# An output projection whose first four operand rows go through Strassen's seven products, added up in the output's PSUM banks

## The chip, the cores and the metric

One core of one Trainium2 chip runs the whole kernel. The metric is the device time in microseconds (us) from start to end of one execution; the median of three runs is compared. PE is TensorE (matmul), PEld its weight load, DVE is VectorE, ACT is ScalarE, POOL is GpSimd, SP is SyncE, which issues most transfers.

## What is computed

The reference is a trunk of two layers on 512 tokens of width 1024, all in float32. Each layer has a token mixer and a SwiGLU FFN, with normalisation, shift, scale and gate around them. The change is in the second layer's mixer, a Mamba-2 state-space mixer, and there in its last line:

```python
def ssd_mixer(h, w_in, conv_w, conv_b, dt_bias, a_log, d_skip, norm_g, w_out):
    z, xbc, dt_raw = jnp.split(h @ w_in, [M_D_INNER, M_D_INNER + M_CONV_DIM], axis=-1)
...
    y = ssd_chunked(xs, dt, a, bm, cm) + d_skip.reshape(g, r)[:, :, None] * xs
    y = y.reshape(bsz, s, M_D_INNER) * jax.nn.silu(z)
    y = rms_normalize(y.reshape(bsz, s, g, M_D_INNER // g)).reshape(bsz, s, M_D_INNER) * norm_g
    return y @ w_out
```

The mixer works on eight groups of heads; group g gives the columns 256 g to 256 g + 255 of y, so two of the sixteen rows of 128 that the last product sums over.

## The kernel before

**The product.** `y @ w_out` sums over K = 16 rows (blocks of 128). A row k has an operand y_k of 128 x 512 tokens (`ygs[k]`) and a weight row of 128 x 1024. The output is 512 tokens by 1024 columns: two halves of columns (hf 0 and 1) by four token tiles of 128, eight tiles of 128 x 512, and each fills one PSUM bank, of which there are eight: four with the tag mm, four with the tag aux. Half 0 lies in the mm banks, half 1 in the aux banks. Float32 accuracy comes from splitting each operand into a high part, rounded by ACT, and a low part, the rest, by DVE (`split_w` L212 for weights, `y_act` L1959 for y), and three matmuls: high by high, high by low, low by high. So one row costs 8 tiles x 3 matmuls of 128x512 (`mm_tiles`, L381; its matmul is L388).

**Staging.** `out_begin` (L375) makes two generators, one for each half. Each step loads up to four weight rows (`load_wo`, L237) into one of two 8 KB tiles wst, hands out the list of split operations, and on the next step issues the matmuls. The split weights lie in four tiles whl. Half 0 takes rows 0 to 13, half 1 rows 0 to 11; the rest (14, 15 and 12 to 15) are the tail, which the class `Boundary` (L409) issues tile by tile, so that the normalisation and the transposes for the FFN (L509) run between them, in the order written out in `BOUNDARY` (L362). The split y of rows below 12 is made twice, once for each half; those from 12 on are kept.

**The order around it.** The state-space groups run in a software pipeline: the loop over g = 1 to 6 projects group g + 1, finishes group g and normalises group g - 1 (`root`, two ACT functions, and `norm` on DVE). A group's sums of squares come from PE (`sums`, tile ssg in an aux bank) and `root` reads them. `step_a` (L1765) transposes into four aux banks (xtok twice, btokp, cb); `states` takes two, `step_cc` four (yo, yd). After the loop, group 7 is finished among the rows of half 0: rows 0 to 3, `step_a`, rows 4 to 7, `states`, rows 8 to 11, `step_cc`, rows 12 and 13, `sums`; then half 1 and the boundary. In this stretch the text of the kernel gives the order of PE, ACT and DVE up to the last `norm`, and then of PE alone up to the boundary, which again gives all three; otherwise a planner orders the instructions. A tile or bank that is used again waits for the last reader of what was in it.

**Where the memory comes from.** The pool sp holds the group's tiles. When it is closed, a pool bp of 13 tiles of 4 KB takes its place, for the gate, the FFN's first split weights (`load_lead`, L259) and the like. x, which the boundary needs, is loaded again from a copy in HBM into the tiles x0 to x3 behind the loop (L2124).

Of the kernel before, what the change touches and what calls it, by code (L numbers as in the profile page):

```python
# [8 lines left out]
F32 = mybir.dt.float32  # L9
F32R = mybir.dt.float32r  # L10
# [6 lines left out]
P = 128  # L17
T = 512
# [20 lines left out]
def trunk_kernel(  # L39
# [197 lines left out]
    def load_wo(m, hf, k0, nk, later=None, stage=None):  # L237


        src = m[k0 * P:(k0 + nk) * P, hf * T:(hf + 1) * T].rearrange("(k p) f -> p k f", p=P)  # L240
        if stage is None:
            st = wst_p.tile([P, 4, T], F32, tag="wst", name="wsto")
            dma(st[:, :nk, :], src)
        res = []
        for k in range(0, nk, 2):
            w = whl_p.tile([P, 2, 2, T], F32R, tag="whl", name="whlo")
            if stage is None:
                sk = st[:, k:k + 2, :]
# [8 lines left out]
        return res  # L257

    def load_lead(srcs, tile4, later=None):  # L259
# [112 lines left out]
""".split()  # L372
    LATE = 3

    def out_begin(s, w, get_act, K, gg, xn_tile, first, lead, after, stage=None, ys=None, held=None, values=()):  # L375

        ys = [None, None] if ys is None else ys
        held = {} if held is None else held
# [2 lines left out]
        def mm_tiles(hf, ks, tiles, get=get_act):  # L381
            for k, wt, kk in ks:
                a = get(k)
                for t in tiles:
                    tk = slice(t * P, (t + 1) * P)
                    pst = ys[hf][t]
                    for i, (al, wl) in enumerate(((0, 0), (0, 1), (1, 0))):
                        pe.matmul(pst, a[:, al, tk], wt[:, wl, kk, :], start=k == 0 and i == 0,  # L388
                                  stop=k == K - 1 and i == 2, skip_group_check=bool(held))

        def pieces(hf):
            kl = K - (2, 4)[hf]
            k = 0
            while k < kl:
                n = min(4, kl - k)
                ops, acts = [], {}
                ks = load_wo(w, hf, k, n, ops, stage if hf else None)
# [5 lines left out]
                if k == 0:  # L403
# [1221 lines left out]
    with ExitStack() as ph:  # L1625
# [96 lines left out]
        class Group:  # L1722
# [167 lines left out]
            def sums(self):  # L1890
# [4 lines left out]
                else:  # L1895
                    for i in range(2):
                        pe.matmul(self.ssg, ones_r, self.sqs[:, i, :], start=i == 0, stop=i == 1)

            def root(self):
                self.rg = t2("rg")  # L1900
                act.activation(self.rg, self.ssg, AF.Ln, bias=eps_t, scale=1.0 / 256)
                act.activation(self.rg, self.rg, AF.Exp, scale=-0.5)

# [55 lines left out]
        def y_act(k):  # L1959

            if k in split:
                return split[k]
            a = ysp.tile([P, 2, T], F32R, tag="ys", name="ys")
            act.copy(a[:, 0, :], ygs[k])
            dve.tensor_tensor(a[:, 1, :], ygs[k], a[:, 0, :].bitcast(F32), SUB)  # L1965
            if k >= 12:
                split[k] = a
            return a

        gg2, bp = [], []  # L1970
# [4 lines left out]
        def xn_half():  # L1975
            return yp.tile([P, T], F32, tag="y", name="xn")

        parts = out_begin(2, wm_out, y_act, 16, gg2, lambda: (xn_half(), xn_half()), "mm",
                          all_of(ffn_lead(1, tile4b)), ffn_after(1))

        with tc.manual_schedule(engines={PE_ENGINE, mybir.EngineType.Activation, mybir.EngineType.DVE}):
            cur, nxt, nn = Group(0), Group(1), Group(2)
# [81 lines left out]
            for g in range(1, NG - 1):  # L2064
# [34 lines left out]
                if nn:  # L2099
                    nn.weights(0)  # L2100
                    nn.later[0][0]()
                late_fin()
                cur.step_cc()
                nxt.later[5][1]()
# [16 lines left out]
            assert next(steps_late, 0) == 0  # L2121
            for t in range(4):
                xt[t] = hp.tile([P, D], F32, tag=f"x{t}", name=f"x{t}")
                dma(xt[t], x_d[t])  # L2124
# [9 lines left out]
            for op in ops[3:]:  # L2134
                op()
            next(parts[0])
            cur.e_sub(0)
            for op in next(parts[0]):
# [8 lines left out]
            for op in ops[:3]:  # L2147
                op()
            for q in range(2):
                cur.e_mul(q)  # L2150
            for op in ops[3:]:
                op()
            late_fin()
            assert not fins_late or next(fins_late[0], 0) == 0
            ops = next(parts[1])
            for op in ops[:5]:
                op()
# [6 lines left out]
        for op in ops[5:]:  # L2164
            op()
        with tc.manual_schedule(engines={PE_ENGINE}):
            next(parts[1])
            core.close()
            bp.append(ph.enter_context(tc.tile_pool(name="bp", bufs=13, reuse_waits="tile")))
            gg2.append(make_gg(2, lambda: tile4b([P, D], F32, "gg")))  # L2170
            begun = out_finish(parts)

# [434 lines left out]
```

## Time and profile before

| | us |
|---|---|
| median of three runs | 1317.64 |
| lowest, highest | 1317.07, 1319.29 |
| the profiled execution | 1317.96 |
| its span in the profile | 1316.1 |
| PE busy in the span | 1301.8 |
| out-projection's matmuls on PE, first to last start | 874.5 to 972.1 |

The span begins with the first and ends with the last instruction of the profile. A line of a timeline reads: start, duration, engine, line of the kernel, operation, output <- inputs, shape, count; in brackets the idle time before it and what ended it. Neighbouring matmuls overlap, so the time of one is the distance from start to start.

### The profile page before, as it was taken

Reading aid. Unit: us, or ns where it says so; the run is one execution under the profiler, and the core shown is the slowest. Engines: PE = TensorE matmul, PEld = TensorE weight load, DVE = VectorE, ACT = ScalarE, POOL = GpSimd, SP = SyncE. Lnnn points to the kernel's source line nnn. Section 1 sums busy time; section 2 is a strip of 40 time slices with the busy share of each in tenths; the row PEclk is TensorE's granted clock in tenths of the full one; section 3 lists DMA queues with packets and bytes.
Section 4 is the critical chain, followed back from the end, with each engine's and each line's share of the span. In section 5 each row is a group of like instructions: output and inputs, shape, how many; then the busy total and the mean of one; then the engine's idle time right before and its main releaser. Section 6 shows DMA issues by size and latency. Waiting matters only on the chain.

```text
span 1316.1 us, 20444 instructions
## 1 busy us (share of the span) xinstructions
PE 1301.8 (99%) x7865; PEld 1142.9 (87%) x7865; DVE 1020.2 (78%) x1531; ACT 723.4 (55%) x1257; POOL 113.2 (9%) x139
## 2 busy tenths in 40 slices
PE   8999999999999999999999999999999999999998
PEld 6787889999988888898888888888889999998886
DVE  5577857977866986768998998977577777766888
ACT  5332247455532565656775567746574555544665
POOL 0000000111100230000000000000000111101330
PEclk9999999999999999999999999999999999999999
DMA  9767661799868984437664456523342788878871
GB/s 310 229 216 227 218 214 52 196 226 241 202 191 271 257 159 122 139 126 223 216 223 158 145 169 203 176 81 113 111 130 57 195 212 214 198 194 284 178 129 65
DMA packets 225301, 239.06 MB, mean 182 GB/s; under 512 B 10276, under 2 KB 177076, under 8 KB 224180
## 3 DMA queue, kind: packets, MB, share of 16 engines
q1 hardware_dynamic: 204720, 195.10, 47.8%
q0 software_dynamic: 16480, 31.20, 13.4%
q10 hardware_dynamic: 4004, 11.46, 2.6%
q8 instruction: 62, 1.02, 0.3%
q14 instruction: 35, 0.29, 0.1%
HBM read 203.76 MB, written 4.34 MB: 158 GB/s over the span
## 4 chain that ended last, share of the span: by engine, by line
PE 83%; DVE 7%; DMA 4%; ACT 3%; SPq 2%; issue 1%; ACTq 0%; DVEq 0%; POOLq 0%
PE sA L669 12%; PE y L388 8%; PE ip L286 8%; PE ip L288 8%; PE ip L287 8%; PE sC L669 6%; PE cA L2316 4%; PE cA L1327 3%; PE sB L669 3%; PE li L286 2%; PE li L288 2%; PE li L287 2%; DMA ada_st<-in_ada_w_dram 2%; PE li L951 1%; DVE ada_acc L128 1%
## 5 line engine op out<-in xcount | busy, mean ns | idle before, releaser
L286 PE MATMUL ip<-h,whl 128*128 128x512 f32 x640 | 252.6, 395 | 0.2 <-DVE cv L1051 0.2
L288 PE MATMUL ip<-h,whl 128*128 128x512 f32 x640 | 249.3, 390 | 0.0
L287 PE MATMUL ip<-h,whl 128*128 128x512 f32 x640 | 249.2, 389 | 0.0
L286 PEld LDWEIGHTS ip<-h,whl 128*128 128x128 f32 x640 | 120.2, 188 | 25.8 <-issue 1.8
L288 PEld LDWEIGHTS ip<-h,whl 128*128 128x128 f32 x640 | 120.1, 188 | 25.5
L287 PEld LDWEIGHTS ip<-h,whl 128*128 128x128 f32 x640 | 120.2, 188 | 24.0
L669 PE MATMUL sA<-tq,whl 128*128 128x256 f32 x1008 | 130.7, 283 | 0.1
L669 PEld LDWEIGHTS sA<-tq,whl 128*128 128x128 f32 x1008 | 125.4, 192 | 0.6 <-ACT g L679 0.3
L232 DVE TENSOR_TENSOR whl<-wst,whl 128x1024 fp32r<-128x1024 f32 x70 | 85.2, 1220 | 22.9 <-ACT whl L231 22.9
L128 DVE SCALAR_TENSOR_TENSOR ada_acc<-ada_st,csil,ada_acc 128x1024 f32<-128x1024 f32 x70 | 89.8, 1282 | 7.0 <-DMA ada_st<-in_ada_w_dram 5.7
L388 PE MATMUL y<-whlo,ys 128*128 128x512 f32 x384 | 89.6, 392 | 0.2 <-DVE ys L1965 0.2
L388 PEld LDWEIGHTS y<-whlo,ys 128*128 128x128 f32 x384 | 71.7, 188 | 16.4 <-issue 0.6
L286 PE MATMUL li<-h,whl 128*128 128x256 f32 x288 | 83.5, 290 | 0.0
L288 PE MATMUL li<-h,whl 128*128 128x256 f32 x288 | 81.5, 283 | 0.0
L287 PE MATMUL li<-h,whl 128*128 128x256 f32 x288 | 81.4, 283 | 0.0
L231 ACT CAST whl<-wst 128x1024 fp32r<-128x1024 f32 x70 | 72.7, 1040 | 1.8 <-DMA wst<-in_m_w_in_dram 1.8
L1714 DVE SCALAR_TENSOR_TENSOR cu<-ip,cols,cu 128x511 f32<-128x511 f32 (+2 forms) x84 | 62.7, 747 | 3.4 <-ACT cu L1711 1.4
L2316 PE MATMUL cA<-whlo,ao 128*128 128x512 f32 x264 | 61.0, 390 | 0.4 <-DVE w2h L2524 0.2
L2316 PEld LDWEIGHTS cA<-whlo,ao 128*128 128x128 f32 x264 | 49.3, 188 | 11.5 <-ACT whlo L2281 1.2
L286 PEld LDWEIGHTS li<-h,whl 128*128 128x128 f32 x288 | 55.2, 192 | 0.8 <-issue 0.8
L287 PEld LDWEIGHTS li<-h,whl 128*128 128x128 f32 x288 | 55.2, 192 | 0.0
L288 PEld LDWEIGHTS li<-h,whl 128*128 128x128 f32 x288 | 55.1, 191 | 0.0
(397 smaller groups left out, 2649.1 us busy)
## 6 DMA issues: line engine op xcount, KB each, us to landing
ada_st<-in_ada_w_dram SPq DMA_DIRECT2D x96, 512.0 KB, 5.9
wsu<-in_f_w_in_dram SPq DMA_DIRECT2D x30, 512.0 KB, 5.8
sg<-in_f_w_in_dram SPq DMA_DIRECT2D x56, 256.0 KB, 3.6
wsu<-in_f_w_in_dram SPq DMA_DIRECT2D x56, 256.0 KB, 4.8
wst<-in_m_w_in_dram SPq DMA_DIRECT2D x14, 1024.0 KB, 6.3
wst<-in_f_w_in_dram SPq DMA_DIRECT2D x10, 1024.0 KB, 6.3
wst<-in_m_w_in_dram SPq DMA_DIRECT2D x20, 512.0 KB, 4.8
wst<-in_a_w_in_dram SPq DMA_DIRECT2D x9, 1024.0 KB, 7.0
```

The source lines that it names most:

```text
L128: dve.scalar_tensor_tensor(acc, w, csil[:, k:k + 1], acc, MUL, ADD)
L231: later.append((lambda sw=sw, w=w: act.copy(w[:, 0, :nk, :], sw), lambda sw=sw, w=w: dve.tensor_tensor(w[:, 1, :nk, :], sw, w[:, 0, :nk, : ...
L232: lambda sw=sw, w=w: dve.tensor_tensor(w[:, 1, :nk, :], sw, w[:, 0, :nk, :].bitcast(F32), SUB)))
L286: pe.matmul(dst, w_at(w, 0, kk), a[:, 0, sl], start=start, stop=False)
L287: pe.matmul(dst, w_at(w, 0, kk), a[:, 1, sl], start=False, stop=False)
L288: pe.matmul(dst, w_at(w, 1, kk), a[:, 0, sl], start=False, stop=stop)
L388: pe.matmul(pst, a[:, al, tk], wt[:, wl, kk, :], start=k == 0 and i == 0, stop=k == K - 1 and i == 2, skip_group_check=bool(held))
L669: pe.matmul(dst, w[:, wl, k0 + k, :], self.moving(q, k, al), skip_group_check=True, start=q in self.FIRST and k == 0 and i == 0, stop=k == ...
L951: pe.matmul(acc_of(i), w[:, part // 2, k, c0:c0 + P], h[kk][:, part % 2, :], start=(kk, part) == (0, 0), stop=(kk, part) == (KD - 1, 2))
L1327: pe.matmul(bank[r, sub], a[:, al, q, tk], w[:, wl, q, :], start=first and k == 0, stop=False, skip_group_check=True)
L1714: dve.scalar_tensor_tensor(u[:, sft:], pst[:, :T - sft], w[3 - sft], u[:, sft:], MUL, ADD)
L2316: pe.matmul(bank[r][sub], a[:, al, q, tk], w[:, hl, q, :], start=first and k == 0, stop=last and k == 2, skip_group_check=True)
```

## The change

Rows 0 to 3 no longer go through `mm_tiles`. They make two pairs (rows 0, 1 and rows 2, 3). In a pair, the weight rows are four blocks b11, b12 (first row, columns 0 to 511 and 512 to 1023) and b21, b22 (second row); y is a11, a12 (tokens 0 to 255 of the first and second row) and a21, a22 (tokens 256 to 511). The output has four quarters of two banks each: B (half 0, tiles 0 and 1), A (half 0, tiles 2 and 3), C (half 1, tiles 0 and 1), D (half 1, tiles 2 and 3). `PRODUCTS` (L34), which two other stages use already, lists the seven products: into which quarter, which weight block, which y block. Product 1 (b21 by a12) opens B, 0 opens A, 2 opens C and 3 opens D; 4, 5 and 6 add to A. Between them the blocks become their sums and differences: on DVE for y (s1, a21, a11, a12) and for b22 and b11, by adding transfers from POOL (`add_`, L585) for b12 and b21.

The quarters are combined in the banks. A's partial sum of rows 4 to 13 is first copied to two tiles (`kept`), so that products 0, 4, 5 and 6 have its banks. ACT copies A after product 0 (`pa`), and DVE adds that to B; ACT copies D after product 3 (`pd`), DVE takes A after product 4 from it and adds it to C; ACT copies minus A after product 5 (`less`), and DVE adds it to D; at the end DVE adds `kept` to A. Plain rows of half 1 stand between the products: 4-5, 6-7, 8-9, 10-11, in pairs.

Around this, the order changes. The weight rows 0 to 3 are loaded into x0 to x3; the loads of x follow late, from POOL. `step_a` follows product 1, and the `root` and `norm` of group 6 follow `states`. The sums of group 7 are copied out of their bank (`keep`). The split y of rows 4 to 11 is kept in the tiles of h, and made once. The pool bp has 14 tiles and is opened earlier; the FFN's first weights are loaded earlier and split in an order written out. The text now gives the order of PE, ACT and DVE for the whole stretch.

```diff
+    def load_rows(m, hf, k0, nk, stage=None):
...
+        return [lambda k=k, raw=raw: split(2 * k, raw) for k, raw in enumerate(raws)]
-                        pe.matmul(pst, a[:, al, tk], wt[:, wl, kk, :], start=k == 0 and i == 0,
-                                  stop=k == K - 1 and i == 2, skip_group_check=bool(held))
+                        pe.matmul(pst, a[:, al, tk], wt[:, wl, kk, :], start=i == 0 and k == (opens[hf][t] if opens else 0),
+                                  stop=k == K - 1 and i == 2, skip_group_check=bool(held or opens))
...
+            def keep(self):
+                self.kept = t2("ssk")
+                act.copy(self.kept, self.ssg)
...
+            if k < 12:
+                a = hp.tile([P, 2, T], F32R, tag=f"h{k - 4}", name="ys")
+            else:
+                a = ysp.tile([P, 2, T], F32R, tag="ys", name="ys")
...
+        NPS = 2
+        def w_rows():
+            for k in range(2 * NPS):
+                rows_w.append(hp.tile([P, D], F32, tag=f"x{k}", name="wrow"))
+                dma(rows_w[k], wm_out[k * P:(k + 1) * P, :])
+            for p in range(NPS):
+                add_(b_("b12", p), b_("b11", p))
+        def w_prep(i):
+            w = w_of[i] = whl_p.tile([P, 2, 2, T], F32R, tag="whl", name="whlo")
+            for p in range(NPS):
+                src = b_(PRODUCTS[i][1], p)
+                act.copy(w[:, 0, p, :], src)
+                dve.tensor_tensor(w[:, 1, p, :], src, w[:, 0, p, :].bitcast(F32), SUB)
+        def a_prep(i, tile):
+            a = a_of[i] = tile([P, 2, NPS, 256], F32R, "ao")
...
+        def product(i):
+            r = PRODUCTS[i][0]
+            for sub in range(2):
...
+                for p in range(NPS):
+                    for k, (al, wl) in enumerate(((0, 0), (0, 1), (1, 0))):
+                        pe.matmul(bank, a_of[i][:, al, p, tk], w_of[i][:, wl, p, :],
+                                  start=i < 4 and p == 0 and k == 0, stop=False, skip_group_check=True)
...
+                    w_rows()
...
-                    for op in next(parts[0]):
-                        op()
+                    ys_out[0] = [mm_ps(f"y0{t}") for t in range(2)]
+                    w_prep(1)
+                    a_prep(1, ys_tile)
                 nxt.project_z(1)
                 cur.sums()
...
-            next(parts[0])
-            prev.root()
+            product(1)
+            ys_out[0] += [mm_ps(f"y0{t}") for t in (2, 3)]
             late_fin()
-            prev.norm()
-            ops = next(parts[0])
-            for op in ops[:3]:
+            for op in next(parts[0]):
                 op()
             cur.step_a()
...
             cur.states()
+            prev.root()
             for q in range(2):
                 cur.e_exp(q)
+            prev.norm()
             next(parts[0])
...
+            sums("s1", "a21", "a22", SUB)
+            rows_1 += load_rows(wm_out, 1, 4, 4)
+            w_prep(3)
+            a_prep(3, ys_tile)
+            w_prep(0)
             cur.step_cc()
             next(parts[0])
+            a_prep(0, ys_tile)
+            kept = [t2("hold") for _ in range(2)]
+            for t in range(2):
+                act.copy(kept[t], out_bank("A", t))
+            core.close()
+            bp.append(ph.enter_context(tc.tile_pool(name="bp", bufs=14, reuse_waits="tile")))
+            gg2.append(make_gg(2, lambda: tile4b([P, D], F32, "gg")))
+            rows_1 += load_rows(wm_out, 1, 8, 4, lambda: tile4b([P, 2, T], F32, "wste"))
+            todo, lead = [], ffn_lead(1, tile4b)
+            leads = lead[0](todo)
...
+            ys_out[1] = [None] * 2 + [aux_ps(f"y1{t}") for t in (2, 3)]
+            sums("a21", "a11", "a21", SUB)
+            sums("a11", "s1", "a11", SUB)
+            sums("a12", "a12", "a11", ADD)
+            w_prep(2)
+            a_prep(2, ys_tile)
+            for p in range(NPS):
+                dve.tensor_add(b_("b22", p), b_("b22", p), b_("b12", p))
+                add_(b_("b21", p), b_("b22", p))
+            product(3)
             cur.sums()
+            pd = tile4b([P, 2, T], F32, "pd")
+            for t in range(2):
+                act.copy(pd[:, t, :], out_bank("D", t))
+            cur.keep()
+            product(0)
+            for op in next(parts[1]):
+                op()
+            w_prep(4)
+            a_prep(4, ys_tile)
+            pa = tile4b([P, 2, T], F32, "pa")
+            for t in range(2):
+                act.copy(pa[:, t, :], out_bank("A", t))
+            ys_out[1][:2] = [aux_ps(f"y1{t}") for t in range(2)]
+            product(2)
+            for t in range(2):
+                dve.tensor_add(out_bank("B", t), out_bank("B", t), pa[:, t, :])
+            next(parts[1])
+            for op in next(parts[1]):
+                op()
             cur.root()
+            product(4)
+            for t in range(2):
+                dve.tensor_tensor(pd[:, t, :], pd[:, t, :], out_bank("A", t), SUB)
+            less = tile4b([P, 2, T], F32, "less")
+            for p in range(NPS):
+                dve.tensor_tensor(b_("b11", p), b_("b22", p), b_("b11", p), SUB)
+            w_prep(5)
+            a_prep(5, ys_tile)
+            next(parts[1])
+            for op in next(parts[1]):
+                op()
+            product(5)
+            w_prep(6)
+            a_prep(6, ys_tile)
+            for t in range(2):
+                dve.tensor_add(out_bank("C", t), out_bank("C", t), pd[:, t, :])
+            for t in range(2):
+                act.activation(less[:, t, :], out_bank("A", t), AF.Copy, scale=-1.0)
             cur.norm()
+            for t in range(4):
+                xt[t] = hp.tile([P, D], F32, tag=f"x{t}", name=f"x{t}")
+                pool.dma_start(xt[t], x_d[t])
             next(parts[1])
+            for op in next(parts[1]):
+                op()
+            for op in todo[:4]:
+                op()
+            product(6)
+            for t in range(2):
+                dve.tensor_add(out_bank("D", t), out_bank("D", t), less[:, t, :])
+            tail = [ends[0][0]()]
+            for k in (14, 15):
+                y_act(k)
+            for load in lead[1:]:
+                leads += load(todo)
+            for t in range(2):
+                dve.tensor_add(out_bank("A", t), out_bank("A", t), kept[t])
+            next(parts[1])
+            tail.append([w for part in ends[1] for w in part()])
+            for op in todo[4:]:
+                op()
+            begun = parts[2](tail, leads)
```

More of the change, by code (lines that the diff above doesn't have):

```diff
@@ L257, in load_wo, with split @@
         return res
+    def load_rows(m, hf, k0, nk, stage=None):
+        src = m[k0 * P:(k0 + nk) * P, hf * T:(hf + 1) * T].rearrange("(k p) f -> p k f", p=P)
+        if stage is None:
+            st = wst_p.tile([P, 4, T], F32, tag="wst", name="wsto")
+            dma(st[:, :nk, :], src)
+            raws = [st[:, k:k + 2, :] for k in range(0, nk, 2)]
+        else:
+            raws = [stage() for _ in range(0, nk, 2)]
+            for k, raw in enumerate(raws):
+                dma(raw, src[:, 2 * k:2 * k + 2, :])
+        def split(k, raw):
+            w = whl_p.tile([P, 2, 2, T], F32R, tag="whl", name="whlo")
+            split_w(raw, w, 2)
+            return [(k0 + k, w, 0), (k0 + k + 1, w, 1)]
+        return [lambda k=k, raw=raw: split(2 * k, raw) for k, raw in enumerate(raws)]
     def load_lead(srcs, tile4, later=None):
@@ L373, in trunk_kernel, with out_begin @@
     LATE = 3
-    def out_begin(s, w, get_act, K, gg, xn_tile, first, lead, after, stage=None, ys=None, held=None, values=()):
+    def out_begin(s, w, get_act, K, gg, xn_tile, first, lead, after, stage=None, ys=None, held=None, values=(),
+                  begin=0, fed=None, opens=None):
         ys = [None, None] if ys is None else ys
@@ L2101, in trunk_kernel @@
                     nn.later[0][0]()
+                else:
+                    assert next(steps_late, 0) == 0
+                    w_rows()
                 late_fin()
@@ L2150, in trunk_kernel @@
                 cur.e_mul(q)
-            for op in ops[3:]:
+            for op in ops[1:]:
                 op()
@@ L2154, in trunk_kernel @@
             assert not fins_late or next(fins_late[0], 0) == 0
-            ops = next(parts[1])
-            for op in ops[:5]:
-                op()
+            pair_s["s1"] = t2("s1")
+            sums("s1", "a21", "a22", SUB)
[3 more added lines that the diff above has]
+            w_prep(0)
             cur.step_cc()
             next(parts[0])
-            cur.sums()
-            cur.root()
+            a_prep(0, ys_tile)
+            kept = [t2("hold") for _ in range(2)]
```

62 lines of the change are left out of this document (39 added, 23 removed).

## The prediction

> **What bounds the kernel now.** I read the page first, then the busy time by stretch around the changed stage, then the timelines of TensorE (PE), ScalarE (ACT) and VectorE (DVE) there.
>
> ```profile
> PE 1301.8 (99%) x7865; PEld 1142.9 (87%) x7865; DVE 1020.2 (78%) x1531; ACT 723.4 (55%) x1257; POOL 113.2 (9%) x139
> ```
> ```profile
> core 0: us, PE busy (x) PEld busy (x) DVE busy (x) ACT busy (x) POOL busy (x), PEclk, DMA share, GB/s
> 874.50:954.00 79.50, 79.25 (x384) 64.84 (x383) 52.99 (x77) 47.14 (x75) 0.00 (x0) 1.00 0.34 112
> 954.00:970.00 16.00, 15.44 (x69) 12.48 (x67) 12.55 (x28) 13.04 (x33) 0.00 (x0) 1.00 0.43 138
> 970.00:1010.00 40.00, 39.72 (x327) 39.22 (x328) 30.56 (x61) 24.14 (x53) 1.79 (x2) 1.00 0.22 54
> ```
>
> PE is busy 99% of the span and 79.25 of 79.5 us here, at clock 1.00. So only two things count: matmuls that go, and time in which PE waits. DVE (53 of 79.5) and ACT (47) have room on average; what matters is whether each operand is there on time.
>
> ```profile
> 873.81 0.39 PE L288 MATMUL ip<-h,whl 128*128 128x512 f32 x1
> 874.49 0.61 PE L388 MATMUL y<-whlo,ys 128*128 128x512 f32 x2
> 875.32 10.73 PE L388 MATMUL y<-whlo,ys 128*128 128x512 f32 x46 [0.22 <-DVE ys L1965]
> 885.89 1.03 PE L1779 MATMUL xtok<-ident,xs 128*128 128x128 f32 x8
> 886.76 0.49 PE L1790 MATMUL btokp<-ident,bt 128*128 128x128 f32 x3
> 887.09 1.06 PE L1796 MATMUL cb<-ct,bt 128*128 128x128 f32 x8
> 887.90 11.16 PE L388 MATMUL y<-whlo,ys 128*128 128x512 f32 x48
> 911.22 1.50 PE L1851 MATMUL yo<-ct,prev 128*128 128x128 f32 x12
> 912.65 1.97 PE L1862 MATMUL yd<-csb,xdt 128*64 128x128 f32 x32
> 914.55 5.74 PE L388 MATMUL y<-whlo,ys 128*128 128x512 f32 x24
> 920.32 1.10 PE L1894 MATMUL ssg<-accg,ones 128*128 128x512 f32 x2
> 920.85 48.50 PE L388 MATMUL y<-whlo,ys 128*128 128x512 f32 x210
> 969.91 0.33 PE L509 MATMUL xtr<-ident,xn 128*128 128x128 f32 x1 [0.56 <-ACT xn L500]
> 970.52 0.55 PE L509 MATMUL xtr<-ident,xn 128*128 128x128 f32 x3 [0.28 <-ACT xn L500]
> ```
>
> The reader is to see three losses. The third matmul should start at 874.49 + 2 x 0.23 = 874.95 and starts at 875.32: 0.37 us. At the transposes of the boundary PE waits 0.56 and 0.28 us. Together 1.21 us.
>
> **Part 1: matmuls that go.** Four K-rows cost 4 x 8 banks x 3 = 96 matmuls; the seven products cost 7 x 2 token tiles x 2 pairs x 3 = 84, of the same 128x512 shape. 12 go. Each costs (48.50 - 0.39) / 209 = 0.230 us (0.39 is the pipelined tail of the last: 0.61 less 0.23). **Gain 2.76 us.**
>
> **Part 2: the start.** I now lay each engine's instructions in program order (the text fixes it for PE, ACT and DVE throughout the stage), each beginning when its engine is free and its operands are 0.06 us old; 875.32 above follows the first DVE operand by that (874.58 + 0.69 below).
>
> ```profile
> 870.76 0.58 ACT L1763 ACTIVATE zs<-ip 128x512 f32<-128x512 f32 x1
> 871.23 1.99 ACT L213 CAST whlo<-wsto 128x1024 fp32r<-128x1024 f32 x2
> 873.12 2.18 ACT L1964 CAST ys<-yg 128x512 fp32r<-128x512 f32 x4
> 887.29 0.48 ACT L1791 COPY btok<-btokp 128x384 f32<-128x384 f32 x1 [5.15 <-PE btokp L1790]
> 973.20 0.72 ACT L526 CAST h<-u 128x256 fp32r<-128x256 f32 x2
> ```
> ```profile
> 872.30 2.36 DVE L214 TENSOR_TENSOR whlo<-wsto,whlo 128x1024 fp32r<-128x1024 f32 x2 [1.58 <-ACT whlo L213]
> 874.58 2.49 DVE L1965 TENSOR_TENSOR ys<-yg,ys 128x512 fp32r<-128x512 f32 x4
> 886.53 0.69 DVE L1783 TENSOR_TENSOR xw<-xtok,dte_tok 128x512 f32<-128x512 f32 x1 [2.48 <-PE xtok L1779]
> 887.14 0.68 DVE L1785 TENSOR_TENSOR xdt<-xtok,dt_tok 128x512 f32<-128x512 f32 x1
> 974.00 0.75 DVE L530 TENSOR_TENSOR h<-u,h 128x256 fp32r<-128x256 f32 x2
> ```
>
> Steps in a row take, on ACT, 0.95 us for 1024 columns, 0.54 for 512, 0.31 for 256; on DVE 1.13, 0.61 and 0.33. Product 1 needs two 512-column weight splits and two 256-column operand splits: ACT from 871.23 to 873.0, DVE to 873.9. PE comes at 874.49. The 0.37 us go.
>
> **Part 3: a wait that comes in.** `step_a` now follows product 1 at 874.49 + 12 x 0.230 = 877.25, and `root` of group 6 has moved behind `states`. Until it runs, the sums ssg of group 6 hold one of the four aux banks. `step_a` takes four (xtok, xtok, btokp, cb), so cb must wait for a release. PE reaches cb at 877.25 + 0.87 + 0.33 = 878.45 (starts of the rows above). On ACT the z activation ends about 874.8 (the second z chunk ends at 874.2), two weight splits and four operand splits follow to 878.85, then the btok copy to 879.30: its bank frees cb at 879.36. **Cost 0.91 us.** Should cb be given the first xtok bank instead, DVE has the six low parts until 880.6, then xw and xdt until 881.85: 3.46 us. Zero is excluded only if ssg does hold a bank. I take 0.91: of the two releases it comes first. Behind cb on PE stand all plain rows; their operands are ready by then.
>
> [...] No stretch above shows a clock under 1.00.
>
> **Part 4: the middle.** After cb the plain rows, `states` and `step_cc` need nothing late (the nearest, the first plain operand, is 1.3 us early). PE ends cb at 879.36 + 0.81 = 880.17 and `step_cc` 96 matmuls, 1.24 us of `states` (911.22 - 887.90 - 96 x 0.230) and 3.33 us later, at 906.8; 24 more end at 912.35, product 3 and ssg (0.53) at 915.65, product 0 at 918.40. DVE meanwhile has the work of `step_cc` later than before, since s1 and the low parts for products 3 and 0 stand ahead of it:
>
> ```profile
> 912.68 0.55 DVE L1867 TENSOR_TENSOR y<-yo,ecsb 128x384 f32<-128x384 f32 x1
> 918.09 0.69 DVE L1870 TENSOR_TENSOR yg<-yg,zs 128x512 f32<-128x512 f32 x1
> 919.48 0.69 DVE L1880 TENSOR_TENSOR accg<-accg,sqg 128x512 f32<-128x512 f32 x1 [0.70 <-ACT sqg L1876]
> ```
> ```profile
> L439 DVE TENSOR_TENSOR c<-cC,c x2: 681/686/692, 538.1 to 543.4; 128x512 f32<-128x512 f32 x2
> L2516 ACT COPY c<-cC x2: 577/580/583, 1249.2 to 1249.6; 128x512 f32<-128x512 f32 x2
> ```
>
> In the layout it begins at 907.95, takes 6.1 us as above less one weight split of 1.13 (to 912.93), and with square and sum to 914.37. Two low parts (0.66) and six 256-column sums (6 x 0.33, with 0.15 between) bring it to 917.17; the split of the new a12 follows on ACT and DVE to 918.72. Product 2, due at 918.40, waits **0.38**. Row pair 4-5 of the second half is due 2.76 later, at 921.54; its weight split stands behind the bank copies (0.58 to 0.62 each, two of D and one of ssg) on ACT and ends on DVE at 921.80: **0.32**. Before pair 8-9, due 72 matmuls behind 921.86, at 938.44, DVE has two sums into pd, two into b11, three weight splits, two operand splits and the sum into C, ending 938.84: **0.46**. The other sums in banks (B, D, A) end 0.6 us or more before their next matmul.
>
> No row of before shows DVE writing a bank. The add that reads one (0.686) equals the same add from memory (0.69), so I take 0.69. [...] Below, a write may hide as well as the read does: nothing. Above, read and write may be paid one after the other, 1.37 us; that is a rival.
>
> **Part 5: the boundary.**
>
> ```profile
> 955.11 2.18 ACT L213 CAST whl<-wst 128x512 fp32r<-128x512 f32 x4 [2.77 <-DMA wst<-in_f_w_in_dram]
> 959.15 2.19 ACT L213 CAST whl<-wst 128x512 fp32r<-128x512 f32 x4 [1.28 <-DMA wst<-in_f_w_in_dram]
> 961.25 0.59 ACT L440 ACTIVATE xn<-y 128x512 f32<-128x512 f32 x1
> ```
>
> Now the FFN weights' splits stand among the boundary's squares and push the second one to 961.25, though its matmuls end about 958 (144 of the 210 come before the boundary, which begins at 954.0; 18 follow). That late chain is the 0.56 and 0.28. In the changed order these splits run on ACT from 948.4 to 952.7, ahead of the first boundary matmul at 952.7; what is late next is DVE, whose low parts last to 958.9, and the chain then meets the transposes with no wait but 0.09 at the first h. **Gain 0.84, cost 0.09.**
>
> ```profile
> x<-x_d SPq DMA_DIRECT2D x3, 512.0 KB, 5.4
> wst<-in_f_w_in_dram SPq DMA_DIRECT2D x4, 1024.0 KB, 5.1
> sg<-sg POOLq DMA_DIRECT2D x2, 256.0 KB, 4.2
> ```
>
> The transfers: four rows of 512 KB take the place that the x loads had, long before use. Two adding transfers on POOL's queue at about 850 and two at 920 have over 10 us before their readers. The x loads move from SP to POOL's queue behind these, released at about 937.6 when product 6's operand is split; the first is read at about 959. One after the other at 5.4 they end at 959.2; only the later ones could be late, and those are read later. The third FFN load is issued at 944.35 and lands at 950, needed at 950.5; ACT then has 1.6 us of idle behind it. All this costs nothing; uncovered, each us that the FFN load is over 2 us late would delay the transposes by up to that. `root` moved twice costs ACT two table loads as before, beside plain rows.
>
> **Sum**: -2.76 - 0.37 - 0.84 + 0.91 + 0.38 + 0.32 + 0.46 + 0.09 = **-1.8 us**. PE stays full behind the boundary, so it reaches the end. The profiled execution took 1317.96 us (span 1316.1 and 1.86 around it), 0.3 above the median of three, 1317.64. Set on the median: **1315.8 us**.
>
> **Rivals.**
>
> - *All waits hide* (15%). If cb finds a bank free and the sums keep ahead, the four waits fall away: -2.76 - 1.21 = -4.0 us, 1313.7. For it: DVE's 53 of 79.5 us. Against: the count of the aux banks.
> - *cb waits for xtok* (15%). 3.46 for 0.91 makes -1.8 + 2.55 = +0.7 us, 1318.4. For it: the plan could hand out the oldest bank. Against: btokp is read by one ACT copy, done earlier.
> - *Slower: DVE's writes into banks cost twice* (13%). At 1.37 us for each of ten sums, the wait before pair 8-9 becomes 2.4 us, the low parts of the last rows come 0.9 late and the transposes 1.0: +3.7 on the forecast, +1.9, 1319.5. It decides from about 0.3 us extra a write, where the gain is down to 0.3. For it: ten new instructions on the engine whose queue is the longest from 938 to 959. Against: the bank read at 0.686.
> - *Small delays add up, without one large one* (7%): at 0.10 instead of 0.06 us for each handover, the waits sum to 0.9 more: -0.9, 1316.7.
>
> **How the numbers follow.** The forecast has 50%. Its own range is 1314.9 to 1316.9. The range 1313.6 to 1319.0 leaves out the dearer part of the slower rival and cases worse than all named. A measurement of this kernel tells some 0.2%, 2.6 us, from no change. Faster by more: the first rival and the forecast's better third, 0.32. Slower by more (over 1320.3): the slower rival's dearer part, or it and the xtok bank at once, 0.12. Within: 0.56.
>
> **What would show it.** PE should have 12 fewer matmuls at L388 and product lines together; a wait at cb for ACT's btok (0.9) or DVE's xdt (3.5), none at 875.3; DVE's adds into banks at 0.69; waits of 0.3 to 0.5 ahead of product 2, pair 4-5 and pair 8-9; no wait at xtr. Wrong it would be if PE waits for a transfer, or if the bank adds take over 1 us.

## The result, and the profile after

The changed kernel took 1313.17 us (median of 7 runs, 1312.75 to 1314.51) against 1317.10 (median of 7, 1315.02 to 1319.29): ratio 0.9971, 95% interval 0.9959 to 0.9982. A second measurement gave 1313.19 (median of 11) against 1316.47, ratio 0.9975 (0.9966 to 0.9984). So the gain is 3.3 to 3.9 us, where 1.8 was forecast, and the time lies just below the range (1313.6 to 1319.0). Kernel before and kernel after were profiled once more in that second measurement; where both profiles of a kernel count, the text says "first" and "second".

The busy time in the page of after (first profile), and two stretches of its windows (columns as in the prediction):

```profile
PE 1299.1 (99%) x7853; PEld 1142.2 (87%) x7853; DVE 1029.2 (78%) x1561; ACT 726.7 (55%) x1274; POOL 118.9 (9%) x147
```
```profile
873.74:952.00 78.26, 77.61 (x379) 64.06 (x378) 64.07 (x105) 55.70 (x100) 3.93 (x6) 1.00 0.43 135
952.00:967.85 15.85, 15.85 (x76) 13.12 (x75) 10.98 (x26) 11.54 (x32) 0.00 (x0) 1.00 0.21 67
```

PE has 12 matmuls fewer (7853 for 7865). Ahead of the boundary DVE's work rose from 53 of 79.5 us to 64 of 78.3, and yet PE is idle for only 0.65 us of it, and not at all in the boundary. TensorE's timeline of after:

```profile
873.74 2.89 PE L2058 MATMUL y<-whlo,ao 128*128 128x512 f32 x12
876.47 1.03 PE L1803 MATMUL xtok<-ident,xs 128*128 128x128 f32 x8
877.34 0.49 PE L1814 MATMUL btokp<-ident,bt 128*128 128x128 f32 x3
878.48 1.16 PE L1820 MATMUL cb<-ct,bt 128*128 128x128 f32 x8 [0.65 <-ACT btok L1815]
...
911.60 2.88 PE L2058 MATMUL y<-whlo,ao 128*128 128x512 f32 x12
914.32 1.02 PE L1918 MATMUL ssg<-accg,ones 128*128 128x512 f32 x2
914.77 6.05 PE L2058 MATMUL y<-whlo,ao 128*128 128x512 f32 x24
920.66 5.60 PE L408 MATMUL y<-whlo,ys 128*128 128x512 f32 x24
...
937.03 5.68 PE L408 MATMUL y<-whlo,ys 128*128 128x512 f32 x24
...
965.68 0.60 PE L533 MATMUL xtr<-ident,xn 128*128 128x128 f32 x4
```

The reader is to see one wait in brackets, at cb, with the releaser and nearly the size that were forecast. Product 1 (873.74) runs through, which is the start's loss gone; the transposes (965.68) wait for nothing. And the three waits of the prediction's middle are not there: product 2 begins after the first 12 of the 24 matmuls from 914.77, that is at 920.66 - 12 x 0.227 = 917.94, and pair 4-5 (920.66) and pair 8-9 (937.03) follow without a bracket. Pair 8-9 alone loses 0.13 us from start to start: 0.05 ahead of its first matmul and 0.08 behind it.

I call the *stage* the time from the first output matmul (874.49 in before, 873.74 in after) to the first feed-forward matmul. It took 98.17 us in before's first profile and 94.11 in after's: 4.06 less. The rest of the span differs by 0.7.

### The profile page after: what moved, and what is told of

Same layout as the page of the kernel before. It is cut to its first block, busy times and chain, and to the rows that moved or that the text cites. A ratio compares the mean times of both kernels' runs of the same rounds, so it can differ in the third digit from the quotient of the medians.

```text
span 1311.4 us, 20504 instructions
## 1 busy us (share of the span) xinstructions
PE 1299.1 (99%) x7853; PEld 1142.2 (87%) x7853; DVE 1029.2 (78%) x1561; ACT 726.7 (55%) x1274; POOL 118.9 (9%) x147
## 4 chain that ended last, share of the span: by engine, by line
PE 93%; DVE 2%; ACT 2%; SPq 2%; DMA 1%; issue 0%; DVEq 0%; ACTq 0%
PE sA L693 12%; PE ip L305 11%; PE ip L307 11%; PE ip L306 11%; PE y L408 8%; PE sC L693 6%; PE cA L2477 5%; PE cA L1351 3%; PE sB L693 3%; PE li L305 3%; PE li L307 3%; PE li L306 3%; PE li L975 1%; PE y L2058 1%; PE cD L2477 1%; PE cC L2477 1%
## 5 line engine op out<-in xcount | busy, mean ns | idle before, releaser
L408 PE MATMUL y<-whlo,ys 128*128 128x512 f32 x288 | 67.2, 391 | 0.0
L408 PEld LDWEIGHTS y<-whlo,ys 128*128 128x128 f32 x288 | 53.8, 188 | 11.4 <-issue 0.5
```

Source lines behind the costliest of these rows:

```text
L408: pe.matmul(pst, a[:, al, tk], wt[:, wl, kk, :], start=i == 0 and k == (opens[hf][t] if opens else 0), stop=k == K - 1 and i == 2, skip_gr ...
```

## The experiments

The first two rows are the two kernels themselves; all others are edits of the changed kernel. The stage is from each kernel's own profile.

| kernel | median, us | ratio to before (95%) | stage, us |
|---|---|---|---|
| before again | 1317.30 | 1.0004 (0.9995 to 1.0013) | 97.22 |
| after again | 1313.19 | 0.9975 (0.9966 to 0.9984) | 94.12 |
| plain products in the new order | 1316.67 | 0.9998 (0.9989 to 1.0006) | 96.72 |
| late splits | 1315.22 | 0.9986 (0.9977 to 0.9995) | 95.55 |
| product 1 twice | 1316.00 | 0.9997 (0.9988 to 1.0005) | 96.78 |
| btok by VectorE | 1318.55 | 1.0008 (0.9999 to 1.0017) | 96.90 |
| free bank for cb | 1312.43 | 0.9969 (0.9957 to 0.9980) | 93.25 |
| sums twice | 1315.33 | 0.9989 (0.9981 to 0.9998) | 95.66 |
| btok by VectorE, again | 1318.51 (one run) | | 98.49 |
| btok by VectorE, four times | 1318.76 | 1.0014 (1.0004 to 1.0024) | 98.54 |
| second bank first | 1314.07 | 0.9979 (0.9970 to 0.9989) | 94.70 |

**The order alone, without Strassen.** The four rows run as eight plain block products at the places of the seven; the block sums, the bank copies and the sums into banks are gone.

```diff
+        PLAIN = (("B", "b11", "a11"), ("B", "b21", "a12"), ("C", "b22", "a12"), ("D", "b22", "a22"),
+                 ("A", "b21", "a22"), ("A", "b11", "a21"), ("C", "b12", "a11"), ("D", "b12", "a21"))
...
-            for t in range(2):
-                dve.tensor_add(out_bank("B", t), out_bank("B", t), pa[:, t, :])
...
+            product(7)
```

> The new order is kept, but rows 0 to 3 are multiplied plainly: eight block products in the places of the seven (the eighth behind the seventh), no sums of blocks, no copies of banks, no adds into banks. Theory: PE is the bound and each matmul that goes is worth its 0.227 us, so the twelve come back: the stretch from the first out-projection matmul to the first FFN matmul of the boundary, 94.11 us after the change and 98.16 before, becomes 94.11 + 12 x 0.227 = 96.8, less at most 0.1 for the wait before pair 8-9; the time stays about 1.3 us under before, which is what the new order alone is worth. Rival, the order brings it all: 94.1, and the time stays 4 us under before. Rival, the sums cost a good part of the matmuls' gain in waits: under 96.0.

The stage took 2.61 us more than after's, close to the 12 matmuls' 2.72 less the 0.13 that the changed kernel loses at pair 8-9. So Strassen's sums cost the stage next to nothing, and the new order by itself is worth 0.5 us of stage against before's second profile and 1.45 against its first. In time it isn't shown to be worth anything: the median is 0.04 us under before's, where 1.3 was expected.

**The feed-forward splits late.** Eight of the leading weights' splits go back behind the boundary's first square.

```diff
-            for op in todo[4:]:
-                op()
-            begun = parts[2](tail, leads)
+            def split_later():
+                for op in todo[4:]:
+                    op()
+                yield
+            begun = parts[2](tail, leads, {"sq0_0": (split_later(),)})
```

> Of the change one part is undone: the last eight splits of the FFN's first weights stand behind the boundary's first square, as in before, and not ahead of the boundary. Theory: the waits of PE at the first transposes (before: a distance of 0.945 us ahead of the first and 0.6 among the four, none after) come from these splits, so they come back, and the stretch grows by 0.6 to 1.6 us over 94.11. Rival, the waits went because PE has fewer matmuls ahead or DVE is freer: no wait, 94.1.

The stage rose by 1.45 us, at the high end of what was expected. ACT's timeline and then PE's, of this kernel:

```profile
952.73 4.25 ACT L213 CAST whl<-wst 128x512 fp32r<-128x512 f32 x8
956.88 0.59 ACT L464 ACTIVATE xn<-y 128x512 f32<-128x512 f32 x1
```
```profile
966.38 0.33 PE L533 MATMUL xtr<-ident,xn 128*128 128x128 f32 x1 [0.68 <-ACT xn L524]
967.00 0.55 PE L533 MATMUL xtr<-ident,xn 128*128 128x128 f32 x3 [0.28 <-ACT xn L524]
```

ACT's timeline in after has the same splits and squares as follows:

```profile
946.48 4.26 ACT L213 CAST whl<-wst 128x512 fp32r<-128x512 f32 x8
952.28 0.60 ACT L464 ACTIVATE xn<-y 128x512 f32<-128x512 f32 x1 [1.53 <-PE y L408]
955.00 0.60 ACT L464 ACTIVATE xn<-y 128x512 f32<-128x512 f32 x1 [2.03 <-PE y L408]
```

In after ACT stands idle ahead of the second square and waits for PE; with the splits late it comes to that square at 956.88 for 955.00, some 2 us later counted from the start of the stage, and both waits of the transposes are back.

**Product 1 twice.** Its 12 matmuls are issued two times over (the second time opens its banks anew, so the output stays the same), so that PE comes to the transposes 2.7 us later and ACT's queue can be done by then.

```diff
             product(1)
+            product(1)
```

> Product 1 is issued twice in a row (the second opens its banks anew, so the output is that of the change); 12 matmuls more. Theory: +2.72 us, of which the wait at cb (0.81) hides in them, since ACT's btok copy is done by then: the stretch becomes 94.11 + 1.9 = 96.0 and the wait at cb is gone. Rival, later waits for ACT or DVE set the time of this part: it grows by less than 1 us.

A miss: the stage rose by 2.67, the whole of the 12 matmuls, and the wait at cb stayed. PE's timeline, then ACT's:

```profile
879.03 0.49 PE L1814 MATMUL btokp<-ident,bt 128*128 128x128 f32 x3
880.09 1.16 PE L1820 MATMUL cb<-ct,bt 128*128 128x128 f32 x8 [0.57 <-ACT btok L1815]
```
```profile
879.56 0.48 ACT L1815 COPY btok<-btokp 128x384 f32<-128x384 f32 x1 [2.54 <-PE btokp L1814]
```

ACT had been idle for 2.54 us ahead of the copy, and 0.57 of the 0.65 us in the bracket stayed. So all but 0.08 us of the wait isn't ACT's queue but a round trip: the last transpose, the copy of 0.48 us, and back.

**btok by VectorE.** In group 7 the copy of btok goes to DVE, behind the reads of xtok: the rival in which cb waits for xtok, brought about.

```diff
-                act.copy(self.btok, pt[:, :NCH - 1, :])
+                (dve.tensor_copy if g == NG - 1 else act.copy)(self.btok, pt[:, :NCH - 1, :])
```

> In group 7 alone the copy of btok goes to DVE, behind the parts of xtok, so that the bank that cb waits for comes free only when DVE has been through its low parts and xtok (about 3.5 us after PE arrives, instead of 0.8). Theory: the stretch becomes 94.11 + 2.7 = 96.8, at an unchanged clock. [...] Rival, PE has slack behind cb: less than +2.

PE in its profile:

```profile
881.01 1.13 PE L1820 MATMUL cb<-ct,bt 128*128 128x128 f32 x8 [3.44 <-DVE xdt L1809]
```

The 3.44 us in the bracket are close to the forecast's 3.46 (from start to start the loss is 3.60). The stage rose by 2.79 in this profile; the median rose by over 5. The other executions gave a reason to look at the clock: a mean granted clock of 0.996 to 0.998 in nine of the 11, where after's have 0.998 to 1.000. Two more kernels followed.

> The kernel with the copy of btok on VectorE once more, for its clock. Its profiled execution showed the granted clock at 1.00 behind a gap of TensorE of 3.7 us and a span of 1313.9 us; most of its other executions had a mean clock of 0.996 to 0.998 where the changed kernel's have 0.998 to 1.000, and a median span of 1316.8 us. Theory (a gap of about 3.5 us is at the edge, and in most executions the clock falls for some microseconds behind it): this profile has a span of 1316 to 1317.6 us, and the granted clock is below 1.00 in one stretch behind the gap. Rival (the clock has nothing to do with it; the time is lost at several places): the clock stays at 1.00 behind the gap and a longer span shows in other waits.

> The copy of btok on VectorE, made four times over, so that the gap of TensorE ahead of cb becomes some 1.4 us longer, about 5.1 us. [...] Rival (no clock effect): a span of 1313.9 + 1.4 = 1315.3 us with the clock at 1.00 throughout.

The gap in the same kernel again, and in the one with four copies (its edit: the copy stands in a loop of four):

```profile
882.28 2.05 PE L1820 MATMUL cb<-ct,bt 128*128 128x128 f32 x8 [3.44 <-DVE xdt L1809]
```
```profile
882.27 1.13 PE L1824 MATMUL cb<-ct,bt 128*128 128x128 f32 x8 [3.44 <-DVE xdt L1809]
```

Windows behind the gap, of the first profile, of the same kernel again, and of the one with four copies:

```profile
878.00:882.00 4.00, 0.99 (x9) 1.02 (x10) 3.99 (x8) 4.00 (x11) 0.00 (x0) 1.00 0.42 133
882.00:886.00 4.00, 4.00 (x20) 3.31 (x19) 4.00 (x6) 4.00 (x12) 0.00 (x0) 1.00 0.02 4
```
```profile
882.00:886.00 4.00, 3.72 (x14) 3.37 (x15) 3.16 (x6) 4.00 (x9) 0.00 (x0) 0.57 0.01 4
```
```profile
882.00:886.00 4.00, 3.73 (x15) 3.19 (x16) 3.90 (x9) 4.00 (x9) 0.00 (x0) 0.67 0.01 4
886.00:890.00 4.00, 4.00 (x17) 3.22 (x17) 4.00 (x6) 1.71 (x6) 0.00 (x0) 0.90 0.10 6
```

PEclk, the third figure from the end, is 1.00, 0.57 and 0.67 behind the same gap of 3.44 us. In the profile with 0.57 the eight matmuls of cb take 2.05 us for 1.13 in the first, and the same kernel's stage is 98.49 for 96.90: the clock costs 1.6 us, in some executions and not in others. The four copies did not lengthen the gap: cb had been given the bank of xtok, which xdt frees, not that of btok. So this kernel repeats the gap of 3.44 us, and what a longer one does is not shown. Its span is 1316.8 us, where the rival had 1315.3, and all ten of its executions have a mean clock of 0.996 to 0.998. The gap's 2.79 and the clock's 1.6 us make 4.4 of the more than 5 us by which the median rose; the rest isn't explained, and one execution of the first of these kernels took 1318.78 us at a mean clock of 1.000.

**A free bank for cb.** DVE copies group 6's ssg out of its bank right behind `late_fin`, and `root` reads the copy.

```diff
-                act.copy(self.kept, self.ssg)
+                if self.g == NG - 2:
+                    dve.tensor_copy(self.kept, self.ssg)
+                else:
+                    act.copy(self.kept, self.ssg)
...
-                if self.g == NG - 1:
+                if self.g >= NG - 2:
                     self.ssg = self.kept
...
             late_fin()
+            prev.keep()
```

> VectorE copies group 6's sum of squares out of its bank as soon as it is there, so that cb of group 7 finds a bank that doesn't wait for the copy of btok. Theory (the wait ahead of cb, 0.81 us, is the round trip from the transposes of B through ScalarE's copy back to TensorE, and stands only because cb shares the bank): cb starts right behind the transposes, the stage takes 93.3 to 93.6 us, 0.5 to 0.8 less than after, and the whole kernel is some 0.6 us faster than after. Rival (the wait moves: cb is let go but the next tile, the states' or the first of the next product, waits as long for VectorE, which has one copy of 0.69 us more in front of it): stage 94.0 to 94.8 us.

```profile
877.48 0.49 PE L1814 MATMUL btokp<-ident,bt 128*128 128x128 f32 x3
877.81 1.06 PE L1820 MATMUL cb<-ct,bt 128*128 128x128 f32 x8
878.62 5.72 PE L408 MATMUL y<-whlo,ys 128*128 128x512 f32 x24
```

cb follows the transposes without a bracket, and the stage is 0.87 us shorter. The median is 0.76 below after's of the same set. It is the fastest version here; the intervals of the two overlap, so the step from after to it is shown by the profile rather than by the times.

**Sums twice.** Each of the eight sums into a bank is followed by one more operation on that bank, which adds zero.

```diff
                 dve.tensor_add(out_bank("B", t), out_bank("B", t), pa[:, t, :])
+                dve.tensor_scalar(out_bank("B", t), out_bank("B", t), 0.0, None, ADD)
```

> Each of the eight sums into an output bank is followed by one more VectorE operation on the same bank, which adds zero: the cost of the sums in place is doubled, by about 0.6 to 0.7 us each, 1.3 us for a pair. Theory (the prediction's account of the stage: VectorE has little lead at the products, so the matmuls behind a sum wait for it from about 0.3 us a write on): stage 96.3 to 97.6 us, 2.2 to 3.5 more than after, and no gain over before to speak of. Rival (the sums stand beside plain matmuls that don't need their banks, and VectorE is idle there): stage below 95.1 us, less than 1 us more than after.

The stage rose by 1.54 and the median by 2.1: both theories missed, one on each side. DVE's timeline, then PE's:

```profile
936.16 0.69 DVE L2307 TENSOR_TENSOR y<-y,pd 128x512 f32<-128x512 f32 x1
936.89 0.70 DVE L2308 TENSOR_SCALAR y<-y 128x512 f32<-128x512 f32 x1
937.50 0.69 DVE L2307 TENSOR_TENSOR y<-y,pd 128x512 f32<-128x512 f32 x1
938.22 0.70 DVE L2308 TENSOR_SCALAR y<-y 128x512 f32<-128x512 f32 x1
```
```profile
937.74 0.93 PE L408 MATMUL y<-whlo,ys 128*128 128x512 f32 x3 [0.62 <-DVE y L2308]
938.98 2.34 PE L408 MATMUL y<-whlo,ys 128*128 128x512 f32 x9 [0.32 <-DVE y L2308]
```

Each of the eight sums is followed by 0.6 to 0.7 us more, and 1.3 of the 1.54 us are lost at one place, at pair 8-9. Ahead of the matmuls into the other three quarters PE waits for no sum; the last 0.2 us are lost among the boundary's first transposes.

**The second bank first.** The two sums into C change places.

```diff
-            for t in range(2):
+            for t in (1, 0):
                 dve.tensor_add(out_bank("C", t), out_bank("C", t), pd[:, t, :])
```

> The two sums into quarter C change places: VectorE writes the second bank first. The prediction set the end of both sums against the first matmul of pair 8-9 and got a wait of 0.46 us; the changed kernel waits 0.08. Theory (each bank waits for its own sum alone, and the prediction counted the pair as one): now the first matmul, into the first bank, has to wait for the later of the two sums, which ends at 937.48 where the matmul is due at 936.96; it waits 0.5 to 0.6 us, and the stage takes 94.5 to 94.7 us, 0.4 to 0.6 more than after. Rival (the sums were simply early enough, in either order): the wait stays at 0.1 us or less and the stage at 94.1 us.

```profile
938.54 2.74 PE L408 MATMUL y<-whlo,ys 128*128 128x512 f32 x11 [0.48 <-DVE y L2306]
```

The stage rose by 0.59. With the order as in the change each bank's matmuls wait only for that bank's sum, and the first is done 0.6 us before the second; the other way round, the wait comes that the prediction had booked.

**Before and after once more.**

> The kernel before, profiled and timed beside the others of this set, as the yardstick. The stage from the first plain output matmul of the first half to the first feed-forward matmul at its end took 98.17 us in the profiled execution of before, and the rest of the span 1217.97 us, some 0.8 us more than in every other kernel's profile here (1216.3 to 1217.3). Theory (that execution was long outside the stage by chance): stage 98.0 to 98.3 us again, rest near 1217.1 us, ratio to before 1.000. Rival (the stage itself differs between executions by a microsecond): a stage of 97.5 us or less, and then the gain of the change that the two first profiles gave, 4.06 us, is partly chance.

> The changed kernel, profiled and timed beside the others of this set. Theory: stage 94.0 to 94.2 us, as in its first profile (94.11), and a median 3.5 to 4.2 us below before's. Rival (the gain differs between chips, since the kernels with parts undone gained 1 us less in time than in their stage): the median stands only 2 to 3 us below before's, with a stage of 94.1 us all the same, and then the loss lies outside the stage.

After repeated itself to 0.02 us. Its median stood 3.28 us below before's, between what the theory and the rival had. Before did not repeat itself, as its rival had foreseen: its stage was 97.22, 0.95 us shorter than in the profile that the prediction was made from. All of that lies in the boundary. ACT's timeline and PE's, of before's second profile:

```profile
956.72 2.18 ACT L213 CAST whl<-wst 128x512 fp32r<-128x512 f32 x4 [0.38 <-DMA wst<-in_f_w_in_dram]
958.81 0.59 ACT L440 ACTIVATE xn<-y 128x512 f32<-128x512 f32 x1
```
```profile
967.70 0.93 PE L509 MATMUL xtr<-ident,xn 128*128 128x128 f32 x4
```

The prediction's row for the same split has 1.28 us of waiting for the transfer. Here the feed-forward weights came 0.9 us earlier; the chain behind them is earlier, and PE loses 0.33 us at the transposes where it lost 1.28. This profile is of the fastest of before's 11 executions there (1315.51 us, median 1317.30). Yet it is the better yardstick. For seven kernels of the table (after again and the edits, without those with btok by VectorE) I compared the gain in stage with the gain in time over the runs of before that were timed beside them: counted from this profile the two agree to 0.5 us, and counted from the first profile the gain in stage is 0.7 to 1.4 us larger.

## Why the prediction fell short

Of the 2.6 us between the forecast, 1315.8, and the measured 1313.17, some 0.5 are the starting point: the forecast was set on 1317.64, the median of three runs, and seven runs of before gave 1317.10. The other 2.1 are the gain, 3.9 where 1.8 was forecast. The steps against the runs, in us of the stage (negative is a gain):

| step | predicted | before's first profile | before's second |
|---|---|---|---|
| 12 matmuls | -2.76 | -2.72 | -2.72 |
| the start | -0.37 | -0.49 | -0.49 |
| around ssg of group 7 | none | -0.53 | -0.52 |
| boundary: transposes, first h | -0.75 | -1.28 | -0.33 |
| cb | +0.91 | +0.87 | +0.87 |
| product 2 | +0.38 | 0 | 0 |
| pair 4-5 | +0.32 | 0 | 0 |
| pair 8-9 | +0.46 | +0.13 | +0.13 |
| sum | -1.8 | -4.02 | -3.06 |

The stage differs by -4.06 and -3.10. (The measured entries are extra distances from start to start over 0.227 us, one by one; cb's is the stage of after less that with the free bank.)

**Right**: the matmuls, the start, the move of the splits, that ssg holds a bank and cb therefore waits for btok, and the price of a sum in a bank. At cb the size is right partly by luck: Part 3 has ACT's queue hold the copy of btok until 878.85, and the kernel with product 1 twice shows that nearly the same wait stands with ACT idle. DVE's timeline of after:

```profile
912.94 0.69 DVE L1904 TENSOR_TENSOR accg<-accg,sqg 128x512 f32<-128x512 f32 x1 [0.70 <-ACT sqg L1900]
...
917.44 0.75 DVE L2046 TENSOR_TENSOR ao<-yg,ao 128x256 fp32r<-128x256 f32 x2
...
919.31 1.22 DVE L214 TENSOR_TENSOR whlo<-wsto,whlo 128x1024 fp32r<-128x1024 f32 x1
...
936.19 1.29 DVE L2306 TENSOR_TENSOR y<-y,pd 128x512 f32<-128x512 f32 x2
...
949.31 4.90 DVE L214 TENSOR_TENSOR whl<-wst,whl 128x512 fp32r<-128x512 f32 x8
```

Two sums in banks take 1.29 us, 0.69 and 0.60 in a row: as much as DVE's splits of 512 columns in memory (eight take 4.90, which is 0.69 and seven times 0.60).

**Wrong: the middle, Part 4.** "Product 2, due at 918.40, waits 0.38", "0.32" before pair 4-5 and "0.46" before pair 8-9: 1.16 us booked, 0.13 measured. This is the step that failed. Three mistakes lie in it:

- *The end of a pair was set against the first matmul.* Two low parts end at 917.44 + 0.75 = 918.19, after product 2 has begun (917.94), and nothing waits: in `product` the first two matmuls read only y's high part, the third reads the low part of the first pair, ready at 917.86, and the low part of the second pair is read first by the sixth, at 917.94 + 5 x 0.227 = 919.08. By the prediction's own times, too, the operand (918.72) was ready before the sixth matmul (918.40 + 5 x 0.230 = 919.55). Likewise the first sum into C ends at 936.19 + 0.69 = 936.88, ahead of 937.03; the second, at 937.48, belongs to another bank. For pair 8-9 the exchange of the two sums shows it; for product 2 it is read from the rows and from the text of the kernel.
- *PE was put too early.* I gave the sums ssg 0.53 us. From 914.32 to the second matmul of product 0, at 915.41 by its record, are 1.09 us, less one ordinary distance 0.87. So PE comes to product 2 some 0.3 later, and its operands have that much more room. Before has a like loss at its own ssg, so the gain isn't lessened by it.
- *ACT's bank copies were taken too long.* The prediction gives 0.58 to 0.62 us each, and 0.54 for any step of 512 columns in a row. In a row they take 0.48: a pair takes 1.07 where one alone takes 0.60 (below, ACT's timeline of after). Three of them stand ahead of the weight split for pair 4-5, which DVE ends at 919.31 + 1.22 = 920.53, 0.5 before the time that the layout gives (921.80 on before's clock is 921.05 on after's). The copies make 0.2 to 0.4 of that; the rest I have not divided up, so for pair 4-5 the cause is in part open.

```profile
916.66 1.07 ACT L2273 COPY pd<-y 128x512 f32<-128x512 f32 x2
917.61 0.60 ACT L1926 COPY ssk<-ssg 128x512 f32<-128x512 f32 x1
```

**Not booked: 0.53 us around ssg of group 7.** In before, accg ends at 919.48 + 0.69 = 920.17 and PE starts the sums at 920.32, behind it; two plain matmuls after them, at 923.48 and 923.82, are late too, by 0.27 together. In after product 3 stands ahead of the sums, and accg ends at 913.63, 0.7 us early. I had quoted both rows of before and not set the one against the other.

**Mis-sized by chance: the boundary.** -0.75 was the visible waits of one execution, and even there 0.5 too little, since the two bracketed waits (0.56 and 0.28) are less than the extra distances from start to start at the same places (0.72 and 0.56). In another execution it is -0.33. What the change does there is to take ACT's late splits, and with them a late transfer, out of PE's way; how much that is worth differed by about a microsecond between two executions. The 0.09 booked at the first h is not there either: the layout had DVE's low parts last to 958.9, which is 958.15 on after's clock, and they end at 949.31 + 4.90 = 954.21. The timed gains, 3.9 and 3.3, lie between the two sums.

**The rivals.** "All waits hide" came nearest (1313.7 for 1313.17), yet not for its reason: three waits are hidden, the fourth is there, and losses of before that nobody had counted make up for it. "cb waits for xtok" didn't happen; brought about, it gave 1318.55, and the forecast for it was 1318.4. That agreement is partly luck: the forecast to which it adds 2.55 was itself 2.6 us too high, and its sum has nothing for the loss at a lower clock, which is some 1.6 (a stage of 98.49 for 96.90). Behind the same gap of 3.44 us that loss came in two of three profiles, with clocks of 0.57 and 0.67 in the window behind it, and not in the third, with 1.00; from what length of gap on it comes, no run shows. "DVE's writes cost twice" was wrong in the premise (0.69), and its price too: doubled, the sums cost the stage 1.5, not 3.7, so the point from which it decides is far above 0.3 us a write. "Small delays add up" had the wrong sign.

Open: the rest of the span, outside the stage, differs between the profiles by up to 2.0 us (1216.3 to 1218.3), with no edit there; I have not followed it up.

## What to carry to other kernels

When a chain of two halves feeds two banks or two matmul groups, set each half against its own reader: booking the end of the pair against the first reader made waits that didn't exist (at pair 8-9 0.46 us booked, 0.13 measured), and exchanging the halves made that one real (0.59). Before a gain is booked on a wait that ends on a transfer, look at a second execution of the same kernel; here that one wait was worth 0.3 or 1.3 us. And a bank still held by a value that is only read later cost a round trip through another engine at the next reuse: one early copy, on an engine with room, took away 0.87 us.

## What the runs showed of the hardware that was not expected

- A VectorE sum that reads and writes one bank in place takes 0.69 us for 128x512 and 0.60 in a row, as sums in memory do (accg 0.69, two into b22 1.29); ScalarE's copy of 512 columns out of a bank takes 0.48 in a row, less than its cast of as many from memory (0.52: eight take 4.26, one 0.62).
- Behind the same TensorE gap of 3.44 us the granted clock, over the window of 4 us from 882, was 0.57 and 0.67 in two profiles and 1.00 in the third; the stage was 98.49 and 98.54 us in the two, and 96.90 in the third.
- The transfer of the same feed-forward weights held ACT up by 1.28 us in one execution and by 0.38 in another.
